# A hybrid RG-LRU / HGRN2 layer: values computed token by token for two heads at a time, a new order of units, and steps placed by time

## The chip, the cores and the metric

One core of a Trainium2 chip runs the whole program. The metric is the device time of one execution in microseconds, the median of three runs. Engines are named as the profile names them: PE (TensorE, matmuls; PEld is its weight load), DVE (VectorE), ACT (ScalarE), POOL (GpSimd), SP (SyncE, which issues most transfers).

## The reference, cut to what matters

```python
xa, ga, q, ff, fb, v, gb = split(h @ w_in)          # h: 512 latent + 256 context tokens
# group A: conv, gates, linear scans (not touched)
# group B, 16 heads of 128 channels, two directions, chunks of tokens:
f = lb + (1 - lb) * sigmoid(f_pre);  k = 1 - f      # f_pre = ff or fb
scores = einsum('tk,sk,tsk->ts', silu(q), k, decay)
o = scores @ v + (q * exp(F)) @ S                   # S: state, from the context tokens on
S_new = exp(F_last) * S + (k * exp(F_last - F)).T @ v
yb = rmsnorm(o_fwd + o_bwd) * silu(gb)
x = x + gate * (concat([ya, yb]) @ w_out);  return rmsnorm(x)
```

Here `h` is the normalised input, scaled and shifted (adaLN). All inputs are fp32. A matmul of the projections is made of three in fp32r: each operand is split into `hi` and `lo`, and hi x hi, hi x lo and lo x hi are summed.

## The kernel before, in words

**Projection.** `h` stands in SBUF with its 2048 channels on partitions, as 16 blocks of 128 by 768 tokens (256 of the context, then 512 latent). The columns of `w_in` are taken in units of 128. For a unit the weights are stationary and `h` moves: `mm_unit` (L191 to 203) makes, per block of channels, three matmuls of 512 columns where only latent tokens are needed (`q`, `gb`, and A's gate units; L203), and three pairs of 256 and 512 columns where the context is needed too (`ff`, `fb`, `v`; L200 and L201). A unit is 4 tiles of weights of 256 KB; a tile is 4 blocks, and half a tile (2 blocks) is a **slot** of group B. The output, channels by tokens, stands in one of two PSUM tiles `m` of two banks; `evac_b` (L587) takes it out.

**Weights.** For each tile SP loads `wraw` (six buffers), ACT casts it to `whi` (L142), and POOL makes `wlo` as the difference (L143). The loads run some tiles ahead.

**Order.** Group A's units come first. Then each of the 16 heads of group B has the units `q`, `gb`, `ff`, `fb`, `v` (`ORDER_B`, L38), that is 40 slots per head. Behind them comes the output projection (L949) in four quarters of 512 columns, with 32 blocks each; its first quarter runs beside the last steps of head 15.

**Steps of a head.** When `fb` of a head has been evicted, `steps_b` (L617) puts its steps into a table `sched`, by slot numbers that are written out by hand (L577 to 585), counted from the head's first slot; slot 31 is the last of `fb`. `run_slot` calls what stands at a slot when the matmuls of this half have been issued. The steps are: `prep` (slot 33; `kd`, two products into `QQ`), `decay(l)` and `grow(l)` for l = 0 to 6 on DVE (`decay` multiplies `KK` in place, L647, and halves `T`, L651; `grow` writes the next `Q`, which stands by turns in the tiles `QQ` and `ktok`, L666; ACT packs `Kc` and copies the other half), four **visits** at slots 39, 44, 49 and 53, in which PE computes the scores of levels 0 and 1, 2 and 3, 4 and 5, and 6 (L674, L689) and DVE and ACT merge them, `ktr` (slots 55 to 58; 16 DVE transposes of `K` into `ktok`, L575), the transposes of `v` (slots 59 to 62; 16 on DVE into `vtok`), `umm` (64, 66, 68; the states `S`, PE L758), `omm` (70; outputs, L773 to 775, and their norm), `otr` (71; 16 DVE transposes), and `fin` (72; DVE writes `ys` and POOL sends it to `y_d`). The steps of one head so reach into the units of the next one: with 40 slots per head, slot 72 of a head is slot 32 of the next. For the last head the slots behind 56 are stretched (L583). The steps share four PSUM banks `w`.

**Eviction.** `q` and `gb`: ACT sigmoid, DVE product. `ff`, `fb`: ACT sigmoid in two pieces (L569, L570), the affine with the bounds `lb` on DVE (L612, `T`), and K = 1 - T on ACT (L613). `v`: two ACT copies into `vraw` (L597, L598), channels by tokens, which the 16 DVE transposes turn.

**Gate row.** The output gate is a product of a vector with 64 tiles `adag`. From head 1 on, behind five tiles of each head (`GATES`, L579) SP loads one more tile into the ring of `wraw`, and DVE adds it into `gacc` one tile later (`gate_step`, L542; L551, L553). After each 16, five slots later, `go` (L555) sums it over partitions on PE (L559), DVE adds the bias into a tile of `ys` (L561; there is one buffer of `ys`, shared with `fin`), and POOL writes it out.

**Output projection.** `y_conv` (L830) casts `y_d`'s blocks to `yh` (ACT, L837) and `yl` (DVE, L838); block by block PE multiplies them with `w_out` for four groups of tokens; in the first quarter these go to two `m` tiles, two groups in each.

Of the kernel before, what the change touches and what calls it, by code (L numbers as in the profile page):

```python
# [2 lines left out]

# [15 lines left out]
C = 256  # L19
# [4 lines left out]
NH = 16  # L24
# [12 lines left out]
NS = len(START)  # L37
STATS_Q = 2  # L38
ORDER_A = [2] + [cb for h in range(3, NH) for cb in (16 + h, h)]
ORDER_B = [32 + g * 16 + h for h in range(NH) for g in (0, 4, 1, 2, 3)]  # L40


def view(t, off, dims):
# [9 lines left out]
def layer_kernel(ctx: ExitStack, tc, xT, xres, w0, w0e, wi, adas, adag, adagb, wo, par, lw, fw, cst, masks, out):  # L53
# [148 lines left out]
            else:  # L202
                pe.matmul(ph, w, h[:, C:TA], start=s, stop=e)  # L203

    units = [("A", cb) for cb in ORDER_A] + [("B", cb) for cb in ORDER_B]
    NP = 4 * len(units)
    TOT = NP + 4 * 2 * KB
    nxt = {"d": 0, "c": 0}

    def p_dma():  # L210
        i = nxt["d"]
        nxt["d"] += 1
        if i >= TOT:
            return
        wraw[i] = t = wp.tile([128, 4, 128], F32, name="wraw", bufs=6)
        if i < NP:
            n, g = divmod(i, 4)
            sp.dma_start(t, wi[n, :, 4 * g:4 * g + 4, :])
        else:
            q, kb = divmod(i - NP, 2 * KB)  # L220
            sp.dma_start(t.rearrange("p a b -> p (a b)"), wo[q, kb])
# [306 lines left out]

    sched = {}
    slot_now = 0  # L530

    def at(slot, f):
        sched.setdefault(slot, []).append(f)
# [40 lines left out]
            for j in range(4):  # L574
                dve.transpose(dst[32 * j:32 * j + 32, :, 32 * i:32 * i + 32], src[32 * i:32 * i + 32, :, 32 * j:32 * j + 32])  # L575

    PREP, VISIT = 33, {39: (0, 1), 44: (2, 3), 49: (4, 5), 53: (6,)}  # L577
    KTR, VTR, UMM, OMM, OTR, FIN = (55, 56, 57, 58), (59, 60, 61, 62), (64, 66, 68), 70, 71, 72
    GATES = {("ff", 3), ("fb", 0), ("fb", 1), ("fb", 2), ("v", 0)}  # L579

    def put(h, slot, f):
        s = 2 * 20 * h + slot
        if h == NH - 1 and slot > 56:  # L583
            s += (slot - 56) * 4 // 5 + (3 if slot >= UMM[0] else 0)
        at(s, f)

    def evac_b(h, kind, ph):  # L587
        s = bst.setdefault(h, {})
        if kind in ("q", "gb"):
            sg = bq.tile([128, T], F32, name="sg")  # L590
            act.activation(sg, ph[:, 1, :], AF.Sigmoid)
            t = bq.tile([128, T], F32, name=kind, bufs=2)
            dve.tensor_mul(t, ph[:, 1, :], sg)
            s[kind] = t
        elif kind == "v":
            t = bw.tile([128, TA], F32, name="vraw")
            act.copy(t[:, 0:C], ph[:, 0, 0:C])  # L597
            act.copy(t[:, C:TA], ph[:, 1, :])  # L598
            vt = bw.tile([128, 6, 128], F32, name="vtok", bufs=2)
            s["v"] = vt  # L600

            for i, at_ in enumerate(VTR):
                put(h, at_, lambda i=i: transpose(vt, t.rearrange("p (a b) -> p a b", b=128), (i,)))
        else:
            d = 0 if kind == "ff" else 1
            if d == 0:
                s["T"] = bw.tile([128, 2, TA], F32, name="T0")
                s["K"] = bw.tile([128, 2, TA], F32, name="KK")
            f, k = s["T"][:, d, :], s["K"][:, d, :]
            sig2(f, ph)  # L610
            i = 16 * d + h
            dve.tensor_scalar(f, f, lbt[:, 1, i:i + 1], lbt[:, 0, i:i + 1], op0=ALU.mult, op1=ALU.add)  # L612
            act.activation(k, f, AF.Identity, scale=-1.0, bias=ones[:, 0:1])  # L613
            if d == 1:
                steps_b(h)

    def steps_b(h):  # L617
# [177 lines left out]
            del bst[h]  # L795

        put(h, PREP, prep)
        put(h, 34, lambda: (decay(0), grow(0)))
        put(h, 36, lambda: decay(1))
        put(h, 42, lambda: decay(3))  # L800
        for at_, ls in VISIT.items():
            put(h, at_, visit(ls))
        for i, at_ in enumerate(KTR):
# [26 lines left out]
    def y_conv(kb):  # L830
# [7 lines left out]
        dve.tensor_sub(lo, t, hi.bitcast(F32))  # L838
        yhl[kb] = (hi, lo)

    gi = 0
    credit = 0.0
    ph = None
    NA = len(ORDER_A)
    for i in range(NP):
        u, g = divmod(i, 4)
        grp, cb = units[u]
        if u == NA + 2 and g == 3:
            run_steps(len(wq))
            rctx.close()  # L850
            xctx.close()
            rctx = ExitStack()
            bw = rctx.enter_context(tc.tile_pool(name="bw", bufs=1, side="right"))
        p_conv()
        p_dma()
        if i >= NP - 5:
            y_dma(i - NP + 5)
        if i >= NP - 2:
            y_conv(i - NP + 2)
        if grp == "A":  # L860
            full = cb < 16
        else:
            kind = {2: "q", 3: "ff", 4: "fb", 5: "v", 6: "gb"}[cb // 16]
            full = kind in ("v", "ff", "fb")
        if g == 0:
            ph = psm.tile([128, 2, 512], F32, name="m")
        hi, lo = whl.pop(i)
        for k in range(4):
            mm_unit(ph if full else ph[:, 1, :], hi[:, k, :], lo[:, k, :], 4 * g + k, full)
            if k % 2 == 0:  # L870
                continue
            if grp == "A":
                credit += 1.5 if full else 1.0
                while credit >= 1.33:
                    credit -= 1.33
                    run_steps(1)
                continue
            slot_now = 2 * (i - 4 * NA) + (k == 3)
            if u < NA + 3:
                left = 2 * (4 * NA + 10 - i) + (k == 1)  # L880
                run_steps(max(1, -(-len(wq) // max(1, left))))
            run_slot(slot_now)
        if grp == "A":
            if g == 3:
                if cb >= 16:
                    evac_ga(cb - 16, ph[:, 1, :])
                else:
                    evac_xa(cb, ph[:, 0, 0:C], ph[:, 1, :])
                    push_a(cb)
            continue  # L890
        if ("raw", gi) in gst:
            gate_step(gi)
            gi += 1
        if u >= NA + 5 and (kind, g) in GATES:
            gate_raw(gi)
        if g == 3:
            evac_b(cb % 16, kind, ph)

    hctx.close()
    yp1 = ctx.enter_context(tc.tile_pool(name="yp1", bufs=1, side="left"))  # L900
# [38 lines left out]
    for q in range(4):  # L939
        if q % 2 == 0:  # L940
            ms = [psm.tile([128, 2, 512], F32, name="m") for _ in range(2)]
            pos = [ms[t // 2][:, t % 2, :] for t in range(4)]
        else:
            pos = [psw.tile([128, 512], F32, name="w") for _ in range(4)]

        def mm(kb, tk, hi, lo):
            yh, yl = yhl[kb]
            for n, (y, x) in enumerate(((yh, hi), (yh, lo), (yl, hi))):
                pe.matmul(pos[tk], y[:, 128 * tk:128 * tk + 128], wlin(x), start=(kb == 0 and n == 0),  # L949
                          stop=(kb == 2 * KB - 1 and n == 2))  # L950

        tail = []
        for kb in range(2 * KB):
            i = NP + 32 * q + kb
            p_conv()
            p_dma()
            if q == 0:
                slot_now = 2 * (NP - 4 * NA + kb)
                run_slot(slot_now)
                run_slot(slot_now + 1)  # L960
                if not sched and op is None:
                    rctx.close()
                    qctx.close()
                    rctx = ExitStack()
                    yp2 = rctx.enter_context(tc.tile_pool(name="yp2", bufs=1, side="right"))
                    op = rctx.enter_context(tc.tile_pool(name="op", bufs=1, side="right"))
                    ssq = op.tile([128, 4, 4], F32, name="ssq")
                if kb == 0:
                    y_conv(2)
                y_conv(kb + 3)  # L970
                y_dma(kb + 5)
            if kb == (26 if q == 0 else 10):
                gtile, ftile = load_epi(q)
            if pend and kb in (1, 2, 3, 4):
                epi(*pend.pop(0))
            if q == 3 and kb == 12:
                sbias = op.tile([128, 4], F32, name="sbias")
                dve.tensor_reduce(sbias, ssq[:, :, 0:3], axis=mybir.AxisListType.X, op=ALU.add)
                dve.tensor_scalar(sbias, sbias, 1.0 / D, EPS, op0=ALU.mult, op1=ALU.add)
            hi, lo = whl.pop(i)  # L980
            if q == 3 and kb >= 2 * KB - TAIL:
                tail.append((kb, hi, lo))
                continue
            for tk in range(4):
                mm(kb, tk, hi, lo)
        for tk in range(4):
            for kb, hi, lo in tail:
                mm(kb, tk, hi, lo)
            if q < 3:
                pend.append((q, tk, pos[tk]))  # L990
            else:
                rs = finish_a(tk - 1) if tk else None
                epi(q, tk, pos[tk])
                if tk:
                    finish_b(tk - 1, rs)
# [7 lines left out]
def _layout(inputs):  # L1003
# [8 lines left out]
    w = i["w_in"][0].reshape(KB, 128, 112, 128)  # L1012
    a["w0"] = w[:, :, START[:4], :]
    a["w0e"] = w[:, :, START[4:], :]
    a["wi"] = w[:, :, ORDER_A + ORDER_B, :].transpose(2, 1, 0, 3)
    ada = i["ada_w"][0]
    ss = np.stack([ada[:, 0:D].reshape(KB, 128, KB, 128), ada[:, D:2 * D].reshape(KB, 128, KB, 128)], 3)
    a["adas"] = ss.transpose(2, 1, 0, 3, 4).reshape(KB, 128, KB, 256)
# [39 lines left out]
```

## Time and profile before

| | us |
|---|---|
| median of 3 runs | 2310.13 (2308.88 to 2310.85) |
| the profiled execution | 2311.04 |
| its span, first to last instruction | 2309.2 |
| PE busy | 2242.5 |
| DVE busy | 1380.4 |
| ACT busy | 978.6 |
| POOL busy | 966.4 |

The profiled execution is one run with the profiler's records; its span is 1.8 us shorter than its own time, and its time is 0.9 us above the median. A group in the lists gives its busy time and the idle time of its engine just ahead of it. Matmuls are pipelined: the duration of one overlaps with the next, so the time that one costs is read from the distance of two starts. Timelines give start and duration in us, engine, line, operation, what it writes and reads, shape and count; in brackets stands the idle time before it and what ended it.

### The profile page before, as it was taken

How to read it: one execution, taken by the hardware profiler on the slowest of the kernel's cores; microseconds unless marked ns; L12 is line 12 of the kernel's file. 1: busy time of each engine (PE TensorE's matmuls, PEld its weight loads, DVE VectorE, ACT ScalarE, POOL GpSimd, SP SyncE). 2: the span in 40 equal slices, each digit the busy share in tenths (PEclk: the TensorE clock that was granted, in tenths of full speed). 3: DMA queues.
4: the chain of work that ended last, by engine and by line, in shares of the span. 5: the costliest groups of instructions: out<-in, count | busy, mean ns of one | idle time of the engine just before them, and what ended most of it. 6: DMA issues, size and time to landing. Idle time of an engine off the chain costs nothing. (4 is left out here: it accounts for less than half of the span.)

```text
span 2309.2 us, 39194 instructions
## 1 busy us (share of the span) xinstructions
PE 2242.5 (97%) x15550; PEld 1876.8 (81%) x15550; DVE 1380.4 (60%) x2122; ACT 978.6 (42%) x1797; POOL 966.4 (42%) x698
## 2 busy tenths in 40 slices
PE   8999999999999999999999999999999998999998
PEld 4788888888888888888887888888888887788886
DVE  4457666676646776686685586676676667710011
ACT  4357677766633343333333333333334335432222
POOL 2355555555442442443343343243344243465452
PEclk9999999999999999999999999999999999999999
DMA  9942222222122322222222222222222123553443
GB/s 361 363 139 82 83 82 82 83 91 88 65 82 75 92 83 79 87 81 78 82 87 72 80 88 86 70 83 88 78 88 79 59 77 102 161 182 96 123 123 110
DMA packets 121393, 241.97 MB, mean 105 GB/s; under 512 B 13812, under 2 KB 16244, under 8 KB 121208
## 3 DMA queue, kind: packets, MB, share of 16 engines
q1 hardware_dynamic: 118520, 231.06, 31.2%
q0 software_dynamic: 2688, 8.40, 0.9%
q8 instruction: 122, 2.00, 0.3%
q14 instruction: 63, 0.52, 0.1%
HBM read 226.81 MB, written 12.59 MB: 104 GB/s over the span
## 5 line engine op out<-in xcount | busy, mean ns | idle before, releaser
L143 POOL TENSOR_TENSOR wlo<-wraw,whi 128x512 fp32r<-128x512 f32 x556 | 806.2, 1459 | 1156.2 <-ACT whi L142 1071.8
L201 PE MATMUL m<-h,whi 128*128 128x512 f32 x2048 | 763.1, 395 | 0.0
L200 PE MATMUL m<-h,whi 128*128 128x256 f32 x2048 | 581.0, 284 | 0.0
L142 ACT CAST whi<-wraw 128x512 fp32r<-128x512 f32 x556 | 337.9, 621 | 487.8 <-PE m L201 212.7
L201 PEld LDWEIGHTS m<-h,whi 128*128 128x128 f32 x2048 | 384.3, 188 | 86.9 <-issue 1.0
L203 PE MATMUL m<-h,whi 128*128 128x512 f32 x1440 | 454.1, 397 | 0.0
L201 PE MATMUL m<-h,wlo 128*128 128x512 f32 x1024 | 404.8, 395 | 0.0
L200 PEld LDWEIGHTS m<-h,whi 128*128 128x128 f32 x2048 | 386.8, 189 | 9.0 <-issue 6.7
L203 PEld LDWEIGHTS m<-h,whi 128*128 128x128 f32 x1440 | 268.8, 189 | 56.7
L200 PE MATMUL m<-h,wlo 128*128 128x256 f32 x1024 | 288.2, 281 | 0.0
L203 PE MATMUL m<-h,wlo 128*128 128x512 f32 x720 | 282.4, 392 | 0.0
L201 PEld LDWEIGHTS m<-h,wlo 128*128 128x128 f32 x1024 | 192.1, 188 | 46.8
L647 DVE TENSOR_TENSOR KK<-KK,T 128x768 f32<-128x768 f32 x112 | 156.5, 1398 | 66.7 <-PE w L689 61.6
L200 PEld LDWEIGHTS m<-h,wlo 128*128 128x128 f32 x1024 | 193.3, 189 | 0.0
L203 PEld LDWEIGHTS m<-h,wlo 128*128 128x128 f32 x720 | 136.0, 189 | 28.6
L367 DVE SCALAR_TENSOR_TENSOR u<-xp,P,u 128x256 f32<-128x256 f32 x96 | 88.2, 979 | 105.9 <-ACT u L365 105.9
L575 DVE STREAM_TRANSPOSE ktok<-KK 32x384 f32<-32x384 f32 x256 | 145.9, 570 | 3.7
L627 ACT COPY Kc<-KK 128x512 f32<-128x512 f32 x80 | 54.6, 683 | 155.8 <-DVE KK L647 147.3
L765 DVE SCALAR_TENSOR_TENSOR S<-S,T,w 128x128 f32<-128x128 f32 x128 | 44.5, 348 | 122.9 <-PE w L758 88.7
L949 PE MATMUL m<-whi,yh 128*128 128x512 f32 x256 | 101.8, 398 | 6.6 <-ACT vraw L598 5.2
L949 PE MATMUL m<-whi,yl 128*128 128x512 f32 x256 | 100.9, 394 | 2.7 <-DVE yl L838 2.6
L949 PE MATMUL m<-wlo,yh 128*128 128x512 f32 x256 | 100.9, 394 | 0.0
(215 smaller groups left out, 3141.5 us busy)
## 6 DMA issues: line engine op xcount, KB each, us to landing
wraw<-in_wi SPq DMA_DIRECT2D x428, 256.0 KB, 3.2
araw<-in_adas SPq DMA_DIRECT2D x64, 512.0 KB, 7.2
wraw<-in_wo SPq DMA_DIRECT2D x128, 256.0 KB, 2.7
wraw<-in_adag SPq DMA_DIRECT2D x64, 256.0 KB, 2.7
y_d<-ys POOLq DMA_DIRECT2D x32, 256.0 KB, 3.1
wraw<-y_d SPq DMA_DIRECT2D x32, 256.0 KB, 3.0
h<-in_xT SPq DMA_DIRECT2D x16, 384.0 KB, 7.6
wraw<-in_w SPq DMA_DIRECT2D x16, 256.0 KB, 7.7
```

Of the source, the lines that this page charges most:

```text
L142: act.copy(hi, t)
L143: pool.tensor_sub(lo, t, hi.bitcast(F32))
L200: pe.matmul(ph[:, 0, 0:C], w, h[:, 0:C], start=s, stop=e)
L201: pe.matmul(ph[:, 1, :], w, h[:, C:TA], start=s, stop=e)
L203: pe.matmul(ph, w, h[:, C:TA], start=s, stop=e)
L367: dve.scalar_tensor_tensor(dst, xp[:, o + k:o + k + n], cw, dst, op0=ALU.mult, op1=ALU.add)
L575: dve.transpose(dst[32 * j:32 * j + 32, :, 32 * i:32 * i + 32], src[32 * i:32 * i + 32, :, 32 * j:32 * j + 32])
L627: act.copy(Kc[l].rearrange("p c n -> p (c n)").rearrange("p (a b c) -> p a b c", b=2, c=m), view(s["K"], C, [[2 * m, C // m], [TA + m, 2], ...
L647: dve.tensor_mul(kk, kk, view(Tm, 1, [[2, nb // 2], [nb - 1, 2], [0, m]]))
L765: dve.scalar_tensor_tensor(dst, s["S"][:, o + i - 1, :], s["T"][:, d, b:b + 1], pw[:, i, :], op0=ALU.mult, op1=ALU.add)
L949: pe.matmul(pos[tk], y[:, 128 * tk:128 * tk + 128], wlin(x), start=(kb == 0 and n == 0), stop=(kb == 2 * KB - 1 and n == 2))
```

## The change

It does six things.

1. `UNITS_B` replaces `ORDER_B`: the heads go in pairs, with the units `q`, `gb`, `ff`, `fb` of the first, `v` of both, and `q`, `ff`, `fb`, `gb` of the second.
2. The unit `v` covers 256 columns of weights, for two heads, in 8 tiles of 2 blocks each. `mm_v` makes the 128 tokens of each of six groups the stationary operand and lets 256 columns of weights move, so that the output is tokens by channels. It has three PSUM banks: one `m` tile and one of the four `w` banks.
3. The eviction of `v` is six ACT copies into the `vtok` tiles of both heads; `vraw` and the 16 transposes of each head are gone.
4. The affine of `ff` and `fb` runs on ACT.
5. Steps are placed by time: `HALF` gives the planned time of half a tile of each kind, `slot_t` the planned end of each slot, also in the first quarter of the output projection (1.37 per slot), and a step stands at the first slot that ends at or after its time, counted from the end of the head's `fb`.
6. The gate tile behind `v`'s first tile goes behind its fourth, and the start is counted in tiles (20); the weights are laid out in the order of use.

```diff
+CB_B = {"q": 32, "ff": 48, "fb": 64, "v": 80, "gb": 96}
-ORDER_B = [32 + g * 16 + h for h in range(NH) for g in (0, 4, 1, 2, 3)]
+UNITS_B = [(kind, h + (i > 4)) for h in range(0, NH, 2)
+           for i, kind in enumerate(("q", "gb", "ff", "fb", "v", "q", "ff", "fb", "gb"))]
+HALF = {"q": 1.37, "gb": 1.37, "ff": 2.08, "fb": 2.08, "v": 2.12}
...
+    tiles_b = [(kind, h, g) for kind, h in UNITS_B for g in range(8 if kind == "v" else 4)]
...
-            n, g = divmod(i, 4)
-            sp.dma_start(t, wi[n, :, 4 * g:4 * g + 4, :])
+            sp.dma_start(t, wi[i])
...
+    for kind, h, g in tiles_b:
+        for _ in range(2):
+            clk += HALF[kind]
+            slot_t.append(clk)
+        if (kind, g) == ("fb", 3):
+            fb_end[h] = clk
+    for _ in range(2 * 2 * KB):
+        clk += 1.37
+        slot_t.append(clk)
...
-    PREP, VISIT = 33, {39: (0, 1), 44: (2, 3), 49: (4, 5), 53: (6,)}
-    KTR, VTR, UMM, OMM, OTR, FIN = (55, 56, 57, 58), (59, 60, 61, 62), (64, 66, 68), 70, 71, 72
-    GATES = {("ff", 3), ("fb", 0), ("fb", 1), ("fb", 2), ("v", 0)}
+    PREP, GROW, STEP1, STEP3 = 2.5, 4.5, 9.0, 19.0
+    VISIT = {15.5: (0, 1), 23.0: (2, 3), 30.0: (4, 5), 35.0: (6,)}
+    KTR, UMM, OMM, OTR, FIN = (38.0, 40.4, 42.8, 45.2), (50.0, 53.0, 56.0), 60.0, 61.5, 65.5
+    GATES = {("ff", 3), ("fb", 0), ("fb", 1), ("fb", 2), ("v", 3)}
-    def put(h, slot, f):
-        s = 2 * 20 * h + slot
-        if h == NH - 1 and slot > 56:
-            s += (slot - 56) * 4 // 5 + (3 if slot >= UMM[0] else 0)
-        at(s, f)
+    def put(h, us, f):
+        at(bisect_left(slot_t, fb_end[h] + us), f)
...
-            t = bw.tile([128, TA], F32, name="vraw")
-            act.copy(t[:, 0:C], ph[:, 0, 0:C])
-            act.copy(t[:, C:TA], ph[:, 1, :])
-            vt = bw.tile([128, 6, 128], F32, name="vtok", bufs=2)
-            s["v"] = vt
-            for i, at_ in enumerate(VTR):
-                put(h, at_, lambda i=i: transpose(vt, t.rearrange("p (a b) -> p a b", b=128), (i,)))
+            for j in range(2):
+                bst.setdefault(h + j, {})["v"] = bw.tile([128, 6, 128], F32, name="vtok", bufs=2)
+            for n, bank in enumerate(ph):
+                for j in range(2):
+                    act.copy(bst[h + j]["v"][:, 2 * n:2 * n + 2, :],
+                             bank.rearrange("p (a b) -> p a b", a=2)[:, :, 128 * j:128 * j + 128])
...
-            dve.tensor_scalar(f, f, lbt[:, 1, i:i + 1], lbt[:, 0, i:i + 1], op0=ALU.mult, op1=ALU.add)
+            act.activation(f, f, AF.Identity, scale=lbt[:, 1, i:i + 1], bias=lbt[:, 0, i:i + 1])
...
-        put(h, 34, lambda: (decay(0), grow(0)))
-        put(h, 36, lambda: decay(1))
-        put(h, 42, lambda: decay(3))
+        put(h, GROW, lambda: (decay(0), grow(0)))
+        put(h, STEP1, lambda: decay(1))
+        put(h, STEP3, lambda: decay(3))
...
+    def mm_v(banks, hi, lo, kb, k):
+        h_hi, h_lo = hh[kb]
+        for j in range(6):
+            o = banks[j // 2][:, 256 * (j % 2):256 * (j % 2) + 256]
+            for n, (x, w) in enumerate(((h_hi, hi), (h_hi, lo), (h_lo, hi))):
+                pe.matmul(o, x[:, 128 * j:128 * j + 128], wlin(w)[:, 256 * k:256 * k + 256],
+                          start=kb == 0 and n == 0 and j % 2 == 0, stop=kb == KB - 1 and n == 2 and j % 2 == 1)
...
+        if g == 0:
+            ph = psm.tile([128, 2, 512], F32, name="m")
+            if kind == "v":
+                p2 = psw.tile([128, 512], F32, name="w")
+                ph = [ph[:, 0, :], ph[:, 1, :], p2]
+        for k in range(2):
+            if kind == "v":
+                mm_v(ph, hi, lo, 2 * g + k, k)
+            else:
+                full = kind in ("ff", "fb")
+                for j in (2 * k, 2 * k + 1):
+                    mm_unit(ph if full else ph[:, 1, :], hi[:, j, :], lo[:, j, :], 4 * g + j, full)
+            slot_now = 2 * t + k
...
+            run_slot(slot_now)
...
-        if u >= NA + 5 and (kind, g) in GATES:
+        if t >= 20 and (kind, g) in GATES:
             gate_raw(gi)
```

## Rows read from the trace of the kernel before

**Rows 1.** The page: span, and PE's busy time, share and instructions.

```profile
span 2309.2 us, 39194 instructions
...
PE 2242.5 (97%) x15550; PEld 1876.8 (81%) x15550; DVE 1380.4 (60%) x2122; ACT 978.6 (42%) x1797; POOL 966.4 (42%) x698
```

**Rows 2.** PE's waits over the whole span: total us, times, longest us.

```profile
PE w L674 <- DVE ktok L666: 29.5, 27, 3.8
...
PE m L949 <- ACT vraw L598: 5.2, 1, 5.2
...
PE w L674 <- DVE kd L634: 1.0, 1, 1.0
PE w L674 <- DVE QQ L639: 0.8, 1, 0.8
```

**Rows 3.** Timeline of PE, scores of visits 0, 2 and 3 of one head.

```profile
1000.69 0.46 PE L674 MATMUL w<-ktok,Kc 128*32 128x32 f32 x32 [0.62 <-DVE ktok L666]
...
1017.45 0.46 PE L674 MATMUL w<-ktok,KK 128*32 128x32 f32 x32 [1.16 <-DVE ktok L666]
...
1023.50 0.69 PE L689 MATMUL w<-ktok,KK 128*64 128x64 f32 x16
```

**Rows 4.** Timeline of DVE in the same head.

```profile
984.39 5.04 DVE L575 STREAM_TRANSPOSE mg<-kd 32x128 f32<-32x128 f32 x16
...
990.13 0.67 DVE L612 TENSOR_SCALAR T<-T,lbt 128x768 f32<-128x768 f32 x1
...
991.81 0.69 DVE L634 TENSOR_TENSOR kd<-KK 128x512 f32<-128x512 f32 x1 [0.34 <-ACT KK L613]
...
999.49 1.15 DVE L666 TENSOR_TENSOR ktok<-QQ,T 128x512 f32<-128x512 f32 x1 [1.02 <-ACT ktok L665]
1000.48 1.73 DVE L553 SCALAR_TENSOR_TENSOR gacc<-wraw,sc,gacc 128x512 f32<-128x512 f32 x1
```

**Rows 5.** Timeline of DVE, behind a flush of the gate row.

```profile
1250.03 0.68 DVE L561 TENSOR_TENSOR ys<-w,sg 1x512 f32<-1x512 f32 x1 [7.87 <-DMA y_d<-ys]
```

**Rows 6.** Timeline of PE, the second score behind it.

```profile
1257.00 0.65 PE L674 MATMUL w<-ktok,Kc 128*32 128x32 f32 x32 [3.80 <-DVE ktok L666]
```

**Rows 7.** Windows: us, each engine's busy us (count), granted clock, DMA share, GB/s.

```profile
1257.50:1262.00 4.50, 4.50 (x22) 3.50 (x14) 4.50 (x5) 0.79 (x2) 2.15 (x2) 0.50 0.64 176
1934.40:1938.00 3.60, 3.54 (x8) 2.82 (x9) 3.02 (x5) 2.09 (x6) 1.29 (x1) 0.50 0.18 41
```

**Rows 8.** Groups by line: busy us, mean ns, idle before and its releaser.

```profile
L613 ACT ACTIVATE KK<-T,ones 128x768 f32<-128x768 f32 x32 | 30.0, 938 | 100.1 <-DVE T L612 100.1
```

**Rows 9.** Timeline of DVE: merge of visit 2, transposes of `v`.

```profile
1019.91 0.30 DVE L695 COPY_PREDICATED mc<-MK,w 128x128 f32<-128x128 uint8 x1
...
1037.63 6.12 DVE L575 STREAM_TRANSPOSE vtok<-vraw 32x192 f32<-32x192 f32 x16
```

**Rows 10.** Timeline of PE, the first `umm` and the matmul behind it.

```profile
1046.05 1.05 PE L758 MATMUL w<-vtok,ktok 128*128 128x128 f32 x8
1046.86 0.36 PE L200 MATMUL m<-h,whi 128*128 128x256 f32 x1
```

**Rows 11.** Timeline of PE in a `fb`/`v` stretch and in a `q` stretch.

```profile
980.76 0.28 PE L200 MATMUL m<-h,whi 128*128 128x256 f32 x1
980.88 0.40 PE L201 MATMUL m<-h,whi 128*128 128x512 f32 x1
...
984.92 0.28 PE L200 MATMUL m<-h,whi 128*128 128x256 f32 x1
...
1006.65 0.62 PE L203 MATMUL m<-h,whi 128*128 128x512 f32 x2
...
1007.33 0.62 PE L203 MATMUL m<-h,whi 128*128 128x512 f32 x2
```

**Rows 12.** The page's groups: a weight load of the projection.

```profile
L200 PEld LDWEIGHTS m<-h,whi 128*128 128x128 f32 x2048 | 386.8, 189 | 9.0 <-issue 6.7
```

**Rows 13.** Timeline of ACT, the last of the eight `mg` copies of visit 2.

```profile
1022.19 0.30 ACT L703 COPY mg<-mc 32x128 f32<-32x128 f32 x1
```

More of the change, by code (lines that the diff above doesn't have):

```diff
@@ L1 @@
+from bisect import bisect_left
 from collections import deque
@@ L203, in mm_unit @@
                 pe.matmul(ph, w, h[:, C:TA], start=s, stop=e)
-    units = [("A", cb) for cb in ORDER_A] + [("B", cb) for cb in ORDER_B]
-    NP = 4 * len(units)
+    NA = len(ORDER_A)
+    tiles_b = [(kind, h, g) for kind, h in UNITS_B for g in range(8 if kind == "v" else 4)]
+    NP = 4 * NA + len(tiles_b)
     TOT = NP + 4 * 2 * KB
@@ L530, in layer_kernel @@
     slot_now = 0
+    slot_t, fb_end = [], {}
+    clk = 0.0
+    for kind, h, g in tiles_b:
[7 more added lines that the diff above has]
+        slot_t.append(clk)
     def at(slot, f):
@@ L843, in layer_kernel @@
     ph = None
-    NA = len(ORDER_A)
     for i in range(NP):
-        u, g = divmod(i, 4)
-        grp, cb = units[u]
-        if u == NA + 2 and g == 3:
+        if i == 4 * NA + 11:
             run_steps(len(wq))
@@ L859, in layer_kernel @@
             y_conv(i - NP + 2)
-        if grp == "A":
+        hi, lo = whl.pop(i)
+        if i < 4 * NA:
+            u, g = divmod(i, 4)
+            cb = ORDER_A[u]
             full = cb < 16
[L862 to L883, printed above, removed]
+            if g == 0:
+                ph = psm.tile([128, 2, 512], F32, name="m")
+            for k in range(4):
+                mm_unit(ph if full else ph[:, 1, :], hi[:, k, :], lo[:, k, :], 4 * g + k, full)
+                if k % 2:
+                    credit += 1.5 if full else 1.0
+                    while credit >= 1.33:
+                        credit -= 1.33
+                        run_steps(1)
             if g == 3:
@@ L890, in layer_kernel @@
             continue
+        t = i - 4 * NA
+        kind, h, g = tiles_b[t]
+        last = 7 if kind == "v" else 3
+        if g == 0:
+            ph = psm.tile([128, 2, 512], F32, name="m")
+            if kind == "v":
[9 more added lines that the diff above has]
+            slot_now = 2 * t + k
+            if t < 12:
+                left = 2 * (10 - t) + (k == 0)
+                run_steps(max(1, -(-len(wq) // max(1, left))))
+            run_slot(slot_now)
         if ("raw", gi) in gst:
@@ L893, in layer_kernel @@
             gi += 1
-        if u >= NA + 5 and (kind, g) in GATES:
+        if t >= 20 and (kind, g) in GATES:
             gate_raw(gi)
-        if g == 3:
-            evac_b(cb % 16, kind, ph)
+        if g == last:
+            evac_b(h, kind, ph)
     hctx.close()
@@ L957, in layer_kernel @@
             if q == 0:
-                slot_now = 2 * (NP - 4 * NA + kb)
+                slot_now = 2 * (len(tiles_b) + kb)
                 run_slot(slot_now)
@@ L1014, in _layout @@
     a["w0e"] = w[:, :, START[4:], :]
-    a["wi"] = w[:, :, ORDER_A + ORDER_B, :].transpose(2, 1, 0, 3)
+    flat = lambda z: z.transpose(1, 0, 2, 3).reshape(128, -1, 512).transpose(1, 0, 2)
+    cols = [[cb] for cb in ORDER_A]
+    cols += [[CB_B[k] + h, CB_B[k] + h + 1] if k == "v" else [CB_B[k] + h] for k, h in UNITS_B]
+    a["wi"] = np.concatenate([flat(w[:, :, c, :]) for c in cols], 0).reshape(-1, 128, 4, 128)
     ada = i["ada_w"][0]
```

## The prediction

> **What bounds the kernel now.** I read the page's span and engine rows first: TensorE is busy 2242.5 of 2309.2 us [rows 1], so only what lengthens or shortens TensorE's own line can move the end. The second view was the list of TensorE's waits [rows 2]: one entry is large, 29.5 us in 27 waits of the score matmuls (L674) for `ktok` of `grow` (L666) on VectorE, and 1.0 and 0.8 us beside it for `kd` and `QQ`. These are direct losses, since TensorE has no other slack. The third view, its timeline in one head, shows where [rows 3]: 0.62 us at the second score of visit 0, 1.16 us at visit 2, none at visit 3.
>
> The fourth view is VectorE before that visit [rows 4]. At 984.39 it begins 5.04 us of output transposes (`otr`) of the previous head, then the affine of `T` (0.67), and only at 991.81 `prep`; the chain to the end of `grow(0)` takes from there to 1000.64, 8.8 us, and the score starts at 1000.69. Next a gate step (1.73 us) stands ahead of `decay(1)`. So VectorE is late because old work of the last head lies ahead of `prep`. The waits can grow: in one head VectorE stood 7.87 us before L561, for the write of the previous `ys` [rows 5], and TensorE lost 3.80 us [rows 6]. Behind that wait the granted clock was 0.50 for 4.5 us (1.2 instead of 2.4 GHz); the same stands behind a 5.24 us wait at the start of the output projection [rows 7], so a long wait costs about half of such a stretch again.
>
> **Part 1: steps by time.** Positions are counted from the last half of a head's `fb`, with the costs in the diff's own table. Visits 0, 1, 2, 3 stood at 16.6, 23.5, 30.3 and 35.8 us; they now stand at 17.0, 23.3, 31.8, 35.3 in even heads (`v` follows) and 16.4, 23.3, 30.1, 37.0 in odd heads (`gb`, `q`, `gb` follow). So the visits hardly move. What moves is the end of the head before: `omm` stood 2.1 us ahead of the next head's `fb` end, `otr` on that end. Heads are now alternately 78.2 and 66.1 us apart and `omm` stands at 61.5 or 62.0 us. Ahead of odd heads this work is over 10 us before `prep`; ahead of even heads it comes one half, 2.1 us, sooner.
>
> The affine leaves VectorE too: ScalarE does it in about 0.94 us (the neighbouring pass over the same 128x768 takes 938 ns [rows 8]), straight behind the sigmoids, without a hop. Ahead of an even head `prep` then starts 2.1 + 0.67 us and the 0.3 us hop sooner, about 3.1 us; the chain is done 2.5 us ahead of the score that now waits 0.62. In odd heads `K` is ready at most four such passes after `fb`, 3.8 us, so 12.6 us are left to visit 0 for a chain of 8.8. The gate step moves from `v`'s first quarter to its fourth, behind visit 0, so `decay(1)` is ready before visit 0 and the 1.16 us at visit 2, which was this delay handed on, goes as well. Gain: 29.5 + 1.0 + 0.8 and half of the 4.5 us at low clock, **33.5 us**.
>
> What is late next: (a) visit 2 of odd heads, where VectorE has 6.2 us between visits for `grow(3)`, `decay(4)`, `grow(4)`. Bounds 0 and 8 x 1.16 us; I take 3. (b) L561: the gate row is flushed four times, and by the order of the tiles two of the four flushes still meet a previous `ys` whose write has not landed. Bounds 0 and 2 x 5.6 (the 3.80 and the 1.0 and 0.8, which fell in one visit); I take 5, since each comes earlier against its visit than that one. Together **+8 us**, between 0 and 20. (c) `umm` is put 6.2 us sooner. The `K` transposes ended at 1037.63 [rows 9], 8.4 us ahead of `umm` at 1046.05 [rows 10]; the value transposes that filled the rest are gone, so some 2.7 us of slack stay in even heads and 1.5 in odd ones (visit 3 is 0.5 sooner in the one, 1.2 later in the other). I cost that at nothing; uncovered it is what VectorE is late.
>
> **Part 2: no value transposes.** 16 transposes, 6.12 us per head [rows 9], leave VectorE, after the `K` transposes and with nobody waiting: worth nothing itself, but it is what lets `umm` move. The eviction becomes six ScalarE copies per pair where four stood; ScalarE is no bound. One more scratch bank is held through `v` (34 us). Visits 0 to 2 take the other three; I assume that visit 3 then takes the one that has been free longest, at no cost (the other case is a rival).
>
> **Part 3: h stationary.** A pair of heads costs the same columns: 16 blocks x 18 x 256 against 2 x 16 x 3 x (256 + 512). But a half is now 18 loads and matmuls where it was 12. Now: from 980.76 to 984.92 twelve pairs of 256 and 512 columns pass, 0.347 us each, 2.08 us per half [rows 11]. The new half is 18 times the pitch of a 256-column matmul that follows another. No row shows that sequence. Lower bound: half of the 512-column pitch (1006.65 to 1007.33, three matmuls, 0.227 [rows 11]), 0.114 us, 2.05 per half. Upper bound: the 256-column row is followed after 0.12 us (980.76 to 980.88), and a 512-column one takes 0.003 more where a 256-column one comes next (0.347 - 0.117 = 0.230 against 0.227): 0.1225, 2.205 per half. I take 0.1175, near the row of the same size, type and load: 2.115 us, 0.035 more, times 128 halves, **+4.5 us**; the bounds give -4 and +16. That loads keep up is read from `umm`: eight full loads and matmuls of 128 columns pass from 1046.05 to 1046.86, 0.101 us each [rows 10], though one load alone lasts 0.189 [rows 12].
>
> The Trainium skill, in "TensorE: Matmul & The Clock Gate", section "The mechanism", speaks against this part: a weight load runs beside matmuls in flight only where its row group differs, and these loads use all rows. The eight `umm` loads disagree with it; what it would make of the time stands in the last rival.
>
> **Part 4: order of units and tail.** The last unit is now `gb` of head 15, not `v`, and `K` of that head is ready some 6 us sooner after `fb`. The 5.24 us wait was for the eviction of `v` behind ScalarE's copies of visit 0 [rows 2]. Now the second bank pair waits for `gb`'s multiplication, which stands on VectorE behind `prep`, `decay(0)`, `grow(0)` (8.8 us), two `yl` and `decay(1)`. Counted with the rows of VectorE here it is done some 6 to 7 us after the projection could start, of which 1.4 us are useful; about as long as today. I take **-1.5 us**; bounds -7 (wait and low clock gone) and +3. Loads keep size and number; SP and POOL issue the same transfers, with the gate load of `v`'s fourth quarter in place of its first, in the same ring; TensorE waits for no weight in today's list, and without that cover it would.
>
> **Sum.** -33.5 + 8 + 4.5 - 1.5 = -22.5 us. The profiled execution took 2311.0, so 2288.5; the median of the runs is 0.9 lower, so I forecast 2287.
>
> **Rivals.** *The gain is handed on* (0.14). The waits move to visit 2, `umm` and L561 at their bounds, 20 instead of 8, with the pitch up to its upper end: 2296 to 2306. For it: the chain is 8.8 us long [rows 4], so little delay suffices. Against: 6.12 + 2 x 0.67 = 7.5 us per head leave VectorE.
>
> *The third bank* (0.06). If visit 3 gets `v`'s own bank, TensorE must wait for its eviction, which stands on ScalarE behind the `mg` copies: the merge of visit 2 starts 2.0 us after the visit's last score ends (1017.91 [rows 3] to 1019.91 [rows 9]), the copies end near 1022.5 [rows 13], 4.6 us after the score, and six copies more are about 2 us, while TensorE comes after one half of `v` and one of `q`, 3.5 us. That is 3.1 us x 8, +25: 2312, no change. `q` is blocked behind it, as TensorE is in order.
>
> *It does not do what it says* (0.02): VectorE stays late since its operations stretch beside POOL, the waits stay and 4.5 us come on top: 2314.
>
> *Loads that show* (0.10), the slower side. Place: the 18 loads per half of `v`. Price: 6 x 128 = 768 loads more than today, each up to its 0.189 us, 145 us at most, 2432 (2304 x 0.189 = 435 us, 2722, if none overlapped). It decides from a pitch of about 0.127 (22.5 us over 2304 matmuls is 0.010 above my 0.1175); above 0.130 the kernel is slower. A case near the threshold is likelier than the full price: 2315 to 2340. For it: no 256-column matmul in the trace follows another. Against: the eight of [rows 10].
>
> **Numbers.** Forecast 0.68. 0.2% (4.6 us) is about what a measurement of this kernel can tell. Faster is the forecast and the first rival, 0.82; same is the third bank, half of the next and a little of the first, 0.08; slower 0.10. The forecast's own bounds (residual waits 0 to 20, pitch -4 to +16, tail) give 2273 to 2302; with most of the first rival the range is 2273 to 2303.
>
> **What will show it.** Right: the waits of L674 for L666 fall below 8 us; the half of `v` takes 2.1 to 2.15 us; `otr` ends before `prep`; granted clock 1.00 throughout the visits. Wrong: a wait of TensorE for ScalarE at L689, for VectorE at L758, or a pitch in `v` above 0.127.

## The result, and the profile after

| | us |
|---|---|
| median after (4 runs) | 2279.57 (2279.25 to 2279.61) |
| median before (4 runs) | 2310.11 (2308.88 to 2310.85) |
| ratio after / before | 0.9868, 95% interval 0.9851 to 0.9885 |

The change takes 30.5 us off, 1.3%. The forecast was 2287. The page of the profile after:

```profile
span 2277.7 us, 40502 instructions
...
PE 2242.5 (98%) x16318; PEld 1918.2 (84%) x16318; DVE 1236.2 (54%) x1834; ACT 1014.7 (45%) x1845; POOL 955.7 (42%) x698
```

Against [rows 1] the span is 31.5 us shorter and TensorE's busy time is the same to the tenth, with 768 matmuls more. So the sum that went is idle time of TensorE. That the busy time is equal does not mean that each kind of matmul costs what it did: `v` takes more, other groups take less, as the account at the end shows. TensorE's waits after, total us, times, longest:

```profile
PE m L975 <- DVE gb L606: 3.5, 1, 3.5
PE w L769 <- DVE ktok L590: 3.0, 1, 3.0
...
PE m L975 <- DVE yl L849: 1.2, 2, 1.1
...
PE w L685 <- DVE ktok L677: 0.6, 1, 0.6
...
PE m L975 <- ACT yh L848: 0.5, 1, 0.5
```

These answer to [rows 2]. The 29.5 us in 27 waits of the scores for `ktok` are 0.6 us in one; the waits for `kd` and `QQ` are gone. New is one wait of 3.0 us of `umm` (L769) for the `K` transposes. At the output projection four waits of 5.2 us in all stand where four of 9.1 were: the 5.2 of [rows 2], and these two lines of before:

```profile
PE m L949 <- DVE yl L838: 2.6, 2, 2.2
...
PE m L949 <- ACT yh L837: 1.3, 1, 1.3
```

VectorE ahead of an even head, after; start and duration first:

```profile
1139.08 5.05 DVE L590 STREAM_TRANSPOSE mg<-kd 32x128 f32<-32x128 f32 x16
...
1144.83 0.75 DVE L803 SCALAR_TENSOR_TENSOR ys<-mg,P,gb 128x512 f32<-128x512 f32 x1
...
1146.15 3.41 DVE L645 TENSOR_TENSOR kd<-KK 128x512 f32<-128x512 f32 x1
1149.49 0.68 DVE L649 TENSOR_TENSOR QQ<-q,T 128x512 f32<-128x512 f32 x1
1150.09 0.68 DVE L650 TENSOR_TENSOR QQ<-q,T 128x512 f32<-128x512 f32 x1
...
1154.17 1.18 DVE L677 TENSOR_TENSOR ktok<-QQ,T 128x512 f32<-128x512 f32 x1 [1.03 <-ACT ktok L676]
```

This answers to [rows 4]. `otr` ends at 1144.13, a gate step, `fin` and a second gate step follow (2.0 us), `prep` starts at 1146.15, and the last product of `grow(0)` ends at 1155.35. TensorE in the same head:

```profile
1156.17 0.46 PE L685 MATMUL w<-q,kd 128*32 128x32 f32 x32
...
1156.81 0.47 PE L685 MATMUL w<-ktok,Kc 128*32 128x32 f32 x31
```

The score that waited 0.62 us in [rows 3] starts at 1156.81, 1.5 us behind its operand, and waits for nothing. The `v` stretch just ahead of it, first and last row:

```profile
1140.85 0.28 PE L857 MATMUL w<-whi,h 128*128 128x256 f32 x1
...
1143.01 0.28 PE L857 MATMUL w<-whi,h 128*128 128x256 f32 x1
```

Eighteen matmuls lie between the two starts: 2.16 us for a half, 0.120 us each. No row of [rows 11] shows this pitch directly.

### The profile page after: what moved, and what is told of

Its sections match the earlier page's. It is cut to its first block, busy times and chain, and to the rows that moved or that the text cites. A ratio compares the mean times of both kernels' runs of the same rounds, so it can differ in the third digit from the quotient of the medians.

```text
span 2277.7 us, 40502 instructions
## 1 busy us (share of the span) xinstructions
PE 2242.5 (98%) x16318; PEld 1918.2 (84%) x16318; DVE 1236.2 (54%) x1834; ACT 1014.7 (45%) x1845; POOL 955.7 (42%) x698
## 4 chain that ended last, share of the span: by engine, by line
PE 87%; ACT 4%; DVE 4%; issue 3%; POOL 2%; DMA 0%; SPq 0%; ACTq 0%; DVEq 0%; POOLq 0%
PE m L205 21%; PE m L207 18%; PE m L204 11%; PE m L857 8%; PE w L975 8%; PE m L975 7%; PE w L857 4%; PE w L685 2%; PE w L769 2%; PE w L207 2%; PE w L403 2%; PE w L273 1%; POOL i L416 1%; PE w L402 1%; POOL wlo L147 1%
## 5 line engine op out<-in xcount | busy, mean ns | idle before, releaser
L205 PE MATMUL m<-h,whi 128*128 128x512 f32 x1536 | 572.2, 395 | 0.0
L207 PE MATMUL m<-h,whi 128*128 128x512 f32 x1440 | 448.0, 392 | 0.0
L204 PE MATMUL m<-h,whi 128*128 128x256 f32 x1536 | 437.8, 285 | 0.0
L205 PEld LDWEIGHTS m<-h,whi 128*128 128x128 f32 x1536 | 288.3, 188 | 63.5 <-issue 0.5
L207 PEld LDWEIGHTS m<-h,whi 128*128 128x128 f32 x1440 | 268.1, 188 | 55.7 <-issue 0.5
L205 PE MATMUL m<-h,wlo 128*128 128x512 f32 x768 | 303.4, 395 | 0.0
L204 PEld LDWEIGHTS m<-h,whi 128*128 128x128 f32 x1536 | 290.1, 189 | 9.0 <-issue 6.2
L207 PE MATMUL m<-h,wlo 128*128 128x512 f32 x720 | 280.9, 390 | 0.0
L204 PE MATMUL m<-h,wlo 128*128 128x256 f32 x768 | 216.2, 281 | 0.0
L857 PE MATMUL m<-whi,h 128*128 128x256 f32 x1024 | 207.7, 286 | 0.0
L658 DVE TENSOR_TENSOR KK<-KK,T 128x768 f32<-128x768 f32 x112 | 142.6, 1273 | 110.4 <-PE w L685 78.6
L205 PEld LDWEIGHTS m<-h,wlo 128*128 128x128 f32 x768 | 144.0, 188 | 35.0
L857 PEld LDWEIGHTS m<-whi,h 128*128 128x128 f32 x1024 | 168.5, 191 | 1.2 <-issue 0.2
L207 PEld LDWEIGHTS m<-h,wlo 128*128 128x128 f32 x720 | 135.2, 188 | 28.5
L204 PEld LDWEIGHTS m<-h,wlo 128*128 128x128 f32 x768 | 145.0, 189 | 0.0
L857 PE MATMUL m<-wlo,h 128*128 128x256 f32 x512 | 144.8, 283 | 0.0
```

The costliest lines, as they stand in the source:

```text
L204: pe.matmul(ph[:, 0, 0:C], w, h[:, 0:C], start=s, stop=e)
L205: pe.matmul(ph[:, 1, :], w, h[:, C:TA], start=s, stop=e)
L658: dve.tensor_mul(kk, kk, view(Tm, 1, [[2, nb // 2], [nb - 1, 2], [0, m]]))
L857: pe.matmul(o, x[:, 128 * j:128 * j + 128], wlin(w)[:, 256 * k:256 * k + 256], start=kb == 0 and n == 0 and j % 2 == 0, stop=kb == KB - 1 ...
```

## The experiments

Theory and rivals at the start. A: VectorE was late for the visits only because old work lay ahead of `prep`; the token-by-token `v` itself costs some 10 us. B: the gain comes from the 98 us of transposes that leave VectorE. For the size of the cost: F, a fixed part per matmul; N, a part that belongs to `v`'s operands; L, a bound by weight loads.

### The old values with the new steps

The changed kernel, with units, values and eviction of `v` as before; the transposes have times again, and the steps behind them later ones:

```diff
-UNITS_B = [(kind, h + (i > 4)) for h in range(0, NH, 2)
-           for i, kind in enumerate(("q", "gb", "ff", "fb", "v", "q", "ff", "fb", "gb"))]
+UNITS_B = [(kind, h) for h in range(NH) for kind in ("q", "gb", "ff", "fb", "v")]
...
-    KTR, UMM, OMM, OTR, FIN = (38.0, 40.4, 42.8, 45.2), (50.0, 53.0, 56.0), 60.0, 61.5, 65.5
+    KTR, VTR, UMM, OMM, OTR, FIN = (38.0, 40.4, 42.8, 44.5), (46.5, 48.5, 50.5, 52.5), (57.2, 59.3, 61.4), 65.5, 67.6, 71.8
...
-                mm_v(ph, hi, lo, 2 * g + k, k)
+            full = kind in ("ff", "fb", "v")
```

> The value unit as before: one head at a time, channels by tokens, 16 VectorE transposes per head, units in the old order. Kept of the change: affine on ScalarE, steps placed by time with the outputs and otr ahead of the next head's fb end, the gate tile behind v's fourth tile. Theory A (the gain is only that VectorE's old work no longer lies ahead of prep; the token-by-token form itself costs some 10 us): TensorE's waits at L674's counterpart fall from 29.5 to below 5 us, 2268 to 2278 us, at or below the changed kernel's 2279.6. Rival B (the gain is the 98 us of transposes that leave VectorE): waits of 15 us and more stay, 2290 to 2305 us.

Measured 2269.4 us, ratio 0.9816 (0.9799 to 0.9832). TensorE has no wait left at a visit; of the waits in group B and the output projection these remain, all with the last head or behind it:

```profile
PE w L769 <- DVE vtok L589: 3.6, 1, 3.6
PE m L969 <- ACT vraw L610: 2.0, 1, 2.0
PE m L969 <- DVE yl L849: 1.6, 1, 1.6
```

A stands, B falls: with all 98 us of transposes back on VectorE no score waits. The value part of the change, with what hangs on it, costs 10.2 us (2279.57 against 2269.4).

### The affine alone

The kernel before, with one line changed:

```diff
-            dve.tensor_scalar(f, f, lbt[:, 1, i:i + 1], lbt[:, 0, i:i + 1], op0=ALU.mult, op1=ALU.add)
+            act.activation(f, f, AF.Identity, scale=lbt[:, 1, i:i + 1], bias=lbt[:, 0, i:i + 1])
```

> The kernel before with the affine of ff and fb on ScalarE and nothing else. Theory A: K no longer waits for otr, VectorE begins prep some 0.9 us sooner, and a visit that waits about 1.2 us keeps 0.2 to 0.5 of it; the waits of 29.5 us fall to 8 to 15, 2290 to 2300 us. Rival C (only the new place of omm and otr counts, since otr still lies ahead of prep): waits of 25 us and more, 2305 to 2311 us.

Measured 2279.89 us, ratio 0.9867 (0.9853 to 0.9882): the whole gain of the change from one line. The waits:

```profile
PE w L674 <- DVE ktok L666: 8.1, 12, 1.6
```

8.1 us of waits are left, as A has it, but the time fell by 31 us where A's price was 11 to 21. VectorE in the head of [rows 4]:

```profile
978.34 5.04 DVE L575 STREAM_TRANSPOSE mg<-kd 32x128 f32<-32x128 f32 x16
...
984.75 0.69 DVE L634 TENSOR_TENSOR kd<-KK 128x512 f32<-128x512 f32 x1
985.35 2.24 DVE L638 TENSOR_TENSOR QQ<-q,T 128x512 f32<-128x512 f32 x1
987.52 0.68 DVE L639 TENSOR_TENSOR QQ<-q,T 128x512 f32<-128x512 f32 x1
...
991.59 1.18 DVE L666 TENSOR_TENSOR ktok<-QQ,T 128x512 f32<-128x512 f32 x1 [1.01 <-ACT ktok L665]
992.62 1.71 DVE L553 SCALAR_TENSOR_TENSOR gacc<-wraw,sc,gacc 128x512 f32<-128x512 f32 x1
```

`otr` still lies ahead of `prep`, and the gate step still behind `grow(0)`. `prep` comes 6.41 us behind the start of `otr`, where it was 7.42 in [rows 4]: 1.0 us, as counted. The two products of `QQ` then take 2.24 and 0.68 us where they took 1.79 and 1.95. So the chain gains 1.8 us, more than the wait that it caused. Of the 31 us, 21.4 are waits for `ktok` and 1.8 the waits for `kd` and `QQ`. Most of the rest is clock; span and mean granted clock of the kernel before, and then of this one:

```profile
core 0: 2309.2 us, clock 0.994
```

```profile
core 0: 2277.5 us, clock 0.997
```

The clock falls short of full by 0.006 in 2309.2 us, which is 13.9, and by 0.003 in 2277.5, which is 6.8: some 7 us less are lost to the low level, and within the heads no stretch at 0.50 is left. Together 30 us.

### A matmul cut in two

The changed kernel, with `q` and `gb` of group B in two matmuls of 256 columns:

```diff
+            elif split:
+                pe.matmul(ph[:, 0:256], w, h[:, C:C + 256], start=s, stop=False)
+                pe.matmul(ph[:, 256:512], w, h[:, C + 256:TA], start=False, stop=e)
```

> The changed kernel with each 512-column matmul of q and gb in group B as two of 256 columns with the same stationary operand: 1536 matmuls and loads more, columns equal. Theory F (each matmul costs its columns at 2.4 GHz and a fixed 13.5 ns): 1536 x 13.5 ns = 21 us more, 2298 to 2303 us, 256-column pitch 0.120. Rival N (the fixed part belongs to v's operands, a stationary h that changes every matmul): under 6 us more, 2279 to 2286 us.

Measured 2296.75 us, 17.2 more than the changed kernel, 11 ns for each of the 1536 matmuls more; between the two, far nearer to F. The pitch in the stretch:

```profile
1070.09 0.28 PE L208 MATMUL m<-h,whi 128*128 128x256 f32 x1
1070.20 0.28 PE L207 MATMUL m<-h,wlo 128*128 128x256 f32 x1
...
1071.39 0.28 PE L207 MATMUL m<-h,whi 128*128 128x256 f32 x1
```

Eleven matmuls lie between 1070.09 and 1071.39 (the `x1` rows left out among them): 0.118 to 0.120 us each, with the weights of the projection stationary and loaded twice in turn. So the pitch of 0.120 does not belong to `v`'s operands. Cutting 0.227 us [rows 11] in two gives 2 x 0.118 to 2 x 0.120: one matmul more costs 9 to 13 ns by these rows and 11 by the time. Each matmul here has its own weight load, so this is the price of the two together; 256 and 512 columns fit one fixed part.

### 128 columns at a time

The changed kernel, with each matmul of `v` as two of 128 columns (`for c in range(2)` around the call in `mm_v`).

> The changed kernel with v's moving operand cut into 128 columns: 36 matmuls and loads per half, 2304 more in all, columns equal. Theory F without a bound from loads: pitch 0.067 us, 2304 x 13.5 ns = 31 us more, about 2311. Rival L (a load takes as long as the pitch of umm, 0.101 to 0.111 us, and hides only under a matmul that is longer): pitch 0.101 to 0.111, half of v 3.6 to 4.0 instead of 2.16 us, 185 to 235 us more, 2465 to 2515.

Measured 2514.1 us in one run, 235 more. Rows of TensorE, where `x4` counts matmuls:

```profile
1252.34 0.61 PE L858 MATMUL w<-whi,h 128*128 128x128 f32 x4
...
1254.80 0.39 PE L858 MATMUL m<-wlo,h 128*128 128x128 f32 x2
```

Between these two starts lie 22 matmuls in 2.46 us: 0.112 us each, where F has 0.067. F's figure falls and L's upper one stands: at 128 columns something of 0.111 to 0.112 us sets the pitch, and a 256-column matmul (0.120) lies 8 to 9 ns above it. That this something is the load is argued: no run has 128-column matmuls without a load for each. The Trainium skill's "LDWEIGHTS (loading the stationary operand)" in "TensorE: Matmul & The Clock Gate" gives a load's time in ns as columns divided by 1.2, by which 107 ns is an estimate here; the pitch lies 5 ns above it, while the record of a single load is longer, 189 ns [rows 12]. The rule that the prediction took from the Trainium skill's "The mechanism" on the same page, that a load overlaps only where its row group differs, does not hold in any of these runs; the same section also names loads into a background weight buffer.

### The affine back on VectorE

The first experiment took 41 us with the affine, the gate tile and the steps together, the second 31 us with the affine alone; they do not say which part is needed. The theory from here on (D): the chain lacks a microsecond or so, and whatever takes that off frees the visits. Against it (E): the affine made the gain. Here the changed kernel has the line of the second experiment the other way round.

> The changed kernel with the affine of ff and fb back on VectorE, nothing else. Theory D (affine and earlier outputs are two ways to the same margin; each alone frees most visits): odd heads keep no wait, even heads lose the 1.4 us of margin that the changed kernel shows at visit 0 and wait up to 1 us; 2282 to 2289 us, waits of the scores 2 to 10 us. Rival E (the affine alone made the gain): most of the 29.5 us comes back, 2300 to 2312 us.

Measured 2278.41 us, ratio 0.9864 (0.985 to 0.9877): nothing lost, and one score wait of 1.9 us. Both theories' numbers miss; D's mechanism holds further than its price. VectorE, in the even head shown above:

```profile
1145.00 0.68 DVE L623 TENSOR_SCALAR T<-T,lbt 128x768 f32<-128x768 f32 x1
1146.68 0.69 DVE L645 TENSOR_TENSOR kd<-KK 128x512 f32<-128x512 f32 x1 [1.01 <-ACT KK L624]
1147.29 1.79 DVE L649 TENSOR_TENSOR QQ<-q,T 128x512 f32<-128x512 f32 x1
1149.01 1.78 DVE L650 TENSOR_TENSOR QQ<-q,T 128x512 f32<-128x512 f32 x1
...
1154.18 1.20 DVE L677 TENSOR_TENSOR ktok<-QQ,T 128x512 f32<-128x512 f32 x1 [1.00 <-ACT ktok L676]
```

The affine is back, and `prep` waits 1.01 us for `K`. TensorE's score:

```profile
1155.66 0.47 PE L685 MATMUL w<-ktok,Kc 128*32 128x32 f32 x31
```

The chain ends at 1155.38, 0.3 us ahead of it. I had expected the margin of 1.4 us to be used up; it shrank to 0.3, and 0.5 us of what I had missed is that `kd` and the two `QQ` here take 4.26 us where they took 4.77 in the changed kernel.

### Steps and gate without the affine

The first experiment's kernel with the affine on VectorE.

> Old units and old values as in the first run, steps by time and the gate tile behind v's fourth tile, but the affine on VectorE as before: steps and gate alone. Theory D: outputs and otr come 4.2 us sooner than before, so VectorE is free when fb ends; waits of the scores under 3 us, 2268 to 2273 us, as with the affine moved (2269.4). Rival E: 2295 to 2310 us.

Measured 2272.82 us, ratio 0.984 (0.9827 to 0.9854). As D has it: the new places and the gate tile, without the affine, free every visit too, but for one wait of 0.28 us. The new places without the gate tile were not run.

### The affine and the gate tile

The second experiment's kernel with `("v", 3)` for `("v", 0)` in `GATES`.

> The kernel before with the affine on ScalarE and the gate tile of v's first tile behind its fourth. Theory D: the twelve waits that the affine alone leaves (8.1 us, mostly 0.55 us at visit 2) come from the gate step of 1.71 us between grow(0) and decay(1); without it under 2 us are left, 2270 to 2275 us. Rival G (the gate step only moves and delays something else as much): 6 us or more are left, 2278 to 2281 us.

Measured 2270.37 us, ratio 0.9829 (0.9815 to 0.9842). Waits:

```profile
PE w L674 <- DVE ktok L666: 0.7, 1, 0.7
```

0.7 us is left of 8.1. Two lines of the change give 39.5 us; the whole change gives 30.5.

### The gate tile alone

The kernel before with that entry of `GATES` alone.

> The kernel before with the gate tile of v's first tile behind its fourth, nothing else. Theory D (one chain of VectorE, from prep over grow(0) and decay(1) to grow(4), and whatever shortens it by about a microsecond frees the visit that it is late for): the gate step lies behind grow(0), so the wait at visit 0 stays, some 15 x 1.2 us, and the 1.16 us at visit 2 go; 2294 to 2300 us, 14 to 18 us of waits at the scores. Rival H (the two waits are independent of this step): 2306 to 2311.

Measured 2299.47 us, ratio 0.9954 (0.9937 to 0.997), within the forecast:

```profile
PE w L674 <- DVE ktok L666: 18.0, 17, 3.7
```

18.0 us in 17 waits stay; in the heads around 1000 us each is at the second score of visit 0, 0.6 to 1.1 us, and the waits at visit 2 are gone (two of 0.5 are left, in the heads near the end). So the 1.16 us of [rows 3] were handed on through the gate step.

### A version that beats both

The first experiment's kernel with other times for the last head, whose steps share VectorE with `yl`; in two steps, the second (the last pair of lines) moving the states and what follows some 4 us further:

```diff
     def put(h, us, f):
+        if h == NH - 1:
+            us = dict(LATE).get(us, us)
...
-            (50.5, 56.0), (52.5, 58.5), (57.2, 62.5), (59.3, 65.5), (61.4, 68.5), (65.5, 72.0), (67.6, 74.0), (71.8, 78.0)]
+            (50.5, 56.0), (52.5, 58.5), (57.2, 67.0), (59.3, 70.0), (61.4, 73.0), (65.5, 76.5), (67.6, 78.0), (71.8, 82.0)]
```

> The first run's kernel with the last head's steps placed apart: its visit 0 behind the eviction of v, and its transposes, states and outputs spread over the blocks of the output projection, where VectorE also makes yl. The first run lost 2.0, 1.6 and 3.6 us there in three waits, and the clock fell behind them. If these are its last losses: 2259 to 2264 us. If the waits only move within the projection: 2267 to 2271.

Measured 2266.66 us, ratio 0.9814 (0.98 to 0.9827): the wait for the eviction was gone, but two for `yl` of 3.3 us together and one of 3.4 us at `umm` stood; the time lies between the two forecasts, just below the upper one.

> The run before's best kernel with the last head's states, outputs, otr and fin another 4 us later. It still lost 3.4 us at the first umm, for the value transposes, and some time at the lower clock behind it. If VectorE is then done: 2260 to 2263.5 us. If VectorE's yl keep it behind all the same, or y comes too late for the last block: 2265 to 2270.

Measured 2261.73 us, ratio 0.979 (0.9775 to 0.9804), as the first forecast has it. Of the waits on VectorE in the projection one is left:

```profile
PE m L974 <- DVE yl L854: 1.9, 1, 1.9
```

## Why the prediction was right, and where it was not

**The range and the sign** held: 2279.57 in 2273 to 2303. **Mechanism of part 1**: right in that VectorE's chain from `prep` to `grow(0)` ran late because of what lay ahead of it, and that the wait at visit 2 was the same delay handed on. What I had not seen is that the parts of the change overlap. The chain needed some 1 to 2 us: the affine alone gives 31, steps with the gate tile 37, and the gate tile alone 11.4, which is not enough (against medians of before of 2310.8, 2309.9 and 2310.9). They do not add up, because a wait can go only once. The margin came out smaller than counted: in the even head shown `prep` starts 10.66 us ahead of the score that used to wait, where it was 8.26 before without the wait (to 1000.07), so 2.4 us are won of 3.1; and `prep` to `grow(0)` takes 9.2 us instead of 8.8, since `kd` lasts 3.41, though the two `QQ` are short. That leaves 1.5 us, not 2.5.

**What is late next** was the term most mis-sized: +8 us forecast. The 3 us for visit 2 of odd heads did not come; of the 5 us at the flush of the gate row one wait of 0.6 came; and `umm`, costed at nothing, waited 3.0 us once, in the last head, where I had looked at VectorE without the `yl` that share it.

**The pitch of `v`**: +4.5 forecast, 10.2 measured between the changed kernel and the one with the old values; also (2.16 - 2.08) x 128 = 10.2 from the rows. The 10.2 between the kernels is a net figure, though: summed over both traces from each matmul's start to the next one's, `v` takes 281.2 us against 269.2, 12.0 more; the halves of `q` and `gb` take 4.9 less, and the rest, the tail and its clock above all, 2.2 more: 9.3, the difference of the two spans (2277.7 and 2268.5). The step that failed is the choice of 0.1175, because the row is "of the same size, type and load". A start-to-start says what stands between two kinds of matmul, and its row is followed by a 512-column one. The pair, 0.347, less 0.227 leaves 0.120, which is what was measured; that figure was in the rows, between the two ends that I kept. The 0.101 us for `umm` has the same fault: within its eight matmuls the starts lie 0.111 to 0.112 us apart, and only the step to the projection's matmul behind them is 0.03.

**The tail**: -1.5 forecast. The waits fell by 3.9 us, and the longest, 3.5 us, is still the second bank pair, now for `gb`'s product, as part 4 says. The granted clock behind it:

```profile
1899.40:1903.40 4.00, 3.94 (x86) 2.90 (x90) 1.21 (x3) 0.62 (x1) 0.24 (x1) 0.50 0.60 181
```

It is 0.50 for 4 us, as in [rows 7]: the low level, 1.2 GHz. So this stretch is not gained. And a second one stands behind the 3.0 us wait of `umm`, which has no counterpart before:

```profile
1946.00:1950.50 4.50, 4.50 (x15) 3.78 (x14) 2.12 (x5) 0.79 (x2) 0.00 (x0) 0.50 0.78 221
```

So the tail gave about as much as it cost.

**The sum** came out 7.4 us above the measured time. Summed from each matmul's start to the next one's, the traces of before and after give the account: scores 34.3 us less; the other 512-column halves of group B (`q`, `gb`) 7.9 less, some 4 of it low clock; `v` 10.9 more; the rest within 1. So the gain of 33.5 came in full, with its low clock, and some 9 us more, of which nearly 4 lie in `q` and `gb` at the full clock; no run gives a cause for these. The +8 was some 7 too much; against both stand the pitch, 6 too little, and the tail, 1 to 2 too good. That the forecast was only 7.4 us off is thus in part luck: errors on opposite sides met.

**The signs.** The waits at the scores fell to 0.6 us, and the clock was 1.00 from 40 to 1895 us, through the visits of all heads but the last. The half of `v` took 2.16 us, 0.01 above its band. That `otr` ends before `prep` decides nothing, as it did so before ([rows 4]).

**Rivals.** The third bank did not decide: there is no wait at visit 3 (L700) in the list. Loads that show: none at 256 columns; at 128 the pitch has a floor that a load would explain. That the gain is handed on happened only in the last head.

## What to carry to other kernels

A wait of a microsecond that repeats in every round of a pipeline is a chain that is late by a microsecond; look for the cheapest thing ahead of it or on it, move that alone and measure, before the order of the work is rebuilt. Here one line gave what the whole change gave, and two gave more, because the rebuilt part brought its own price. Where columns stay equal and matmuls get more, each one more costs some 11 to 13 ns at 256 and 512 columns in this form, and at 128 columns, each matmul with its load, the pitch did not fall below 0.11 us.

## What was not expected of the hardware

VectorE's product of two 128x512 operands in SBUF takes 0.68 us alone, and mostly much more beside POOL's difference of two. In the changed kernel `kd` took 3.41 us, from 1146.15 to 1149.56; POOL's row of the same time:

```profile
1146.45 2.55 POOL L147 TENSOR_TENSOR wlo<-wraw,whi 128x512 fp32r<-128x512 f32 x2
```

Of the 32 products `QQ` of the changed kernel, the ten that no difference of POOL overlaps took 0.68 us; of the others eighteen took 1.77 to 1.80, and four 0.68 to 0.69, where POOL's own work stretched. The 32 products of `q` and `gb` (L606) have the same shape but read one operand from PSUM; none took more than 0.69, though 14 lay at least 0.6 us beside POOL's difference. One of them, and POOL's row around it:

```profile
1406.11 0.68 DVE L606 TENSOR_TENSOR gb<-m,sg 128x512 f32<-128x512 f32 x1
```

```profile
1402.09 6.50 POOL L147 TENSOR_TENSOR wlo<-wraw,whi 128x512 fp32r<-128x512 f32 x4 [4.42 <-PE m L207]
```

With the affine back on VectorE POOL's pair began when `kd` was all but done, and met the two `QQ` instead (1.79 and 1.78 us). The same three operations thus took 3.61 us (affine alone), 4.26 (affine back), and 4.77 us (changed kernel), by where POOL's work fell. A margin of a microsecond on VectorE is inside this spread; it accounts for 0.8 and 0.5 us in the two experiments whose price was missed while their direction held. It was not tested by moving POOL's work away.
